# A hybrid mLSTM/RWKV-7 decoder step on one core: the scaled input kept in DRAM channel-major, the conditioning weight in wide rows, and pieces handed out more finely

## The chip, the cores and the metric

The kernel runs on one core of a Trainium2 chip. The metric is the device time of one execution in microseconds (us). TensorE (PE in the profile; PEld are its weight loads) does the matrix products, VectorE (DVE) and ScalarE (ACT) the elementwise work, GpSimd (POOL) small helpers, and SyncE (SP) issues all the DMAs, in order, from one queue.

## The reference, cut to what matters

One decoder layer for a prompt of 512 tokens and for 8 sequences of 4 sampled tokens, 1024 channels, in float32:

```python
mod = silu(c) @ w_cond + b_cond                      # [9, 6*1024]
sh1, sc1, g1, sh2, sc2, g2 = split(mod, 6)
h = x * (1 + sc1) + sh1
proj = h @ w_in                                      # mLSTM q, k, v, gates; RWKV r, k, v, LoRA; output gates
y_a = gate_a * head_norm(mlstm(proj)) * mlstm_norm_w   # 4 heads, matrix memory 256 x 256
y_b = (head_norm(rwkv7(proj)) * ... + bonus) * g       # 16 heads, state 64 x 64
y_mix = (y_a + gate_b * y_b) @ w_out
x1 = layer_norm(ALPHA * x + g1 * y_mix)
h2 = x1 * (1 + sc2) + sh2
x2 = layer_norm(ALPHA * x1 + g2 * (relu(h2 @ w_up)**2 @ w_down))
```

The nine rows of `mod` are the prompt's conditioning vector and those of the eight sequences. The outputs are `x2` for both groups and the final states.

## The kernel before

**Layout.** Activations lie channel-major: 128 channels on the partitions, the 32 sample tokens and then the 512 prompt tokens along the free dimension (T = 544; TX = 552 with 8 shift rows in front). Every projection is done in three float32r products: weight and activation are each split in a rounded part and a rest (`hi`, `lo`; ScalarE rounds, VectorE subtracts), and `mm3` (L313 to L315) adds hi*hi, hi*lo and lo*hi. `load_w` loads a weight block of 128 columns into the ring `wring` (two buffers, tile `wraw`) and splits it (L299 `whi`, L301 `wlo`).

**PSUM.** `psA` has two double banks (`big()`) for projections, `psB` four single banks (`tp()`) for everything else: transposes, small products, accumulators.

**Stages.**
1. *Load and conditioning.* `xp` (prompt) and `xs40` (shift rows and sample rows) are loaded and transposed with TensorE into `hf`. The part of `w_cond` for `sh1` and `sc1` (ci 0 to 7, blocks of 256 columns) comes in 16 loads of 512 KB, tile `craw`. `cond` (L339 and following) multiplies a block: 8 contraction tiles, dealt over four column groups of the array (g = 0 to 3, two tiles accumulated in each), a copy `crows`, and two products with `fold`, which sum the four groups and turn channels onto the partitions; VectorE adds the bias and writes `mod`. After each pair of blocks (i, 4 + i) two channel blocks of `hf` are scaled and shifted in place, and split to `hhi` and `hlo`. Behind this stands the first projection (`xsp`), ordered after the last product of `cond`.
2. *RWKV*, eight pairs of heads: `g_proj`, `g_prep`, `g_sample`, `g_inv`, `g_chain`, `g_gate`. `heads_sum` sums over the channels of a head: `parts_of` splits its argument (L562 ScalarE `shi`, L564 VectorE `slo`), then two products with `bones` for each half of the tokens (L568, L569). It is used in `g_prep`, for `sq` and for `bv`. `finish` writes the result of a pair to DRAM, `udr`.
3. *mLSTM*, four heads: `g_mproj`, `g_mcore`, `g_msample` (its accumulator `pacc` keeps a bank of `psB` open over many pieces). In the same stretch of time `g_cond` computes the rest of `mod`, one block of 256 columns at a time (ci 8 to 23): two loads of `craw` (`mp` has two buffers) and one call of `cond`.
4. *Start of the output product*, `g_end`: the pools of the first mLSTM half are closed (`mfront`), prompt and sample rows are loaded once more, `udr` is read back block by block (`uk`, one buffer) and split into `uhi`, `ulo`; in 8 groups of 4 + 1 transposes ALPHA*x is made channel-major, `xt` (L1487 to L1490), and then 12 products over the first 6 contraction tiles of `w_out` begin to add to `xt` (`residual`, L1461 to L1465).
5. *The rest of the output product, layer norm, MLP, layer norm*, written out in order.

**Order of the work.** Stages 2 to 4 are Python generators. Each `yield` gives a due time in nominal us, counted from the generator's base (PP for a pair of heads, MS for an mLSTM projection, CS_ for a conditioning block, ES for an output product); `merge` always resumes the generator whose next piece is due first, at once if its time is already past. So these times only set the program order of the pieces: they are no waits. The tile framework places semaphores and buffers, and may let a ready instruction go ahead of one that is not.

Of the kernel before, what the change touches and what calls it, by code (L numbers as in the profile page):

```python
# [41 lines left out]
def hybrid_kernel(ctx: ExitStack, tc: tile.TileContext, I, O):  # L42
# [127 lines left out]
    def load_x(pool, with_shift):  # L170
        xp = pool.tile([128, 4, D], F32, name="xp")
        dma(xp, I["x_prompt"].rearrange("o (n p) d -> p (o n) d", p=128))
        xs40 = pool.tile([40, D], F32, name="xs40")
        if with_shift:
            dma(xs40[0:NB, :], I["state_rwkv_shift"].rearrange("o b d -> (o b) d"))
        o = 8 if with_shift else 0
        for t in range(NT):
            dma(xs40[o + 8 * t:o + 8 + 8 * t, :], I["x_sample"][:, t, :])
        return xp, xs40
# [12 lines left out]
    def cond_load(ci, pool):  # L192
        raws = []
        for half in range(2):
            raws.append(pool.tile([128, 4, 256], F32, name="craw"))
            dma(raws[half], w_cond[:, 4 * half:4 * half + 4, 256 * ci:256 * ci + 256])
        return raws

    xp, xs40 = load_x(ep, True)
# [30 lines left out]
    for ci in (0, 4, 1, 5, 2, 6, 3, 7):  # L230
        if ci == 3:
            xraw = wring.tile([128, 8, 128], F32, name="wraw")
            dma(xraw, w_in[:, :, OFF_R + 128 * 24:OFF_R + 128 * 25])
        craws[ci] = []
        for half in range(2):
            raw = er.tile([128, 4, 256], F32, name="craw")
            with tc.high_priority() if (ci, half) in ((7,0),(7,1)) else ExitStack():
                dma(raw, w_cond[:, 4 * half:4 * half + 4, 256 * ci:256 * ci + 256])
            craws[ci].append(raw)
# [17 lines left out]
    hf = er.tile([128, 8, TX], F32, name="hf", bufs=1)  # L257
# [75 lines left out]
    def cond(cis, raws, rows, ps, nr=2):  # L333

        n = len(cis)
        for i, ci in enumerate(cis):
            for half in range(2):
                for g in range(4):
                    mm = PE.matmul(ps[32 * g:32 * g + 32, i, :], cth[:, 4 * half + g, :], raws[ci][half][:, g, :],  # L339
                                   start=half == 0, stop=half == 1)  # L340
        rw = rows.tile([128, n, 256], F32, name="crows", bufs=nr)
        S.copy(rw, ps)
        pt = tp([128, n, 2, 9])
        for i, ci in enumerate(cis):
            for j in range(2):
                PE.matmul(pt[:, i, j, :], rw[:, i, 128 * j:128 * j + 128], fold[:, 0:9], start=True, stop=True)
            V.tensor_tensor(mod[:, 2 * ci:2 * ci + 2, :], pt[:, i],
                            bcond[:, 2 * ci:2 * ci + 2].unsqueeze(2).to_broadcast([128, 2, 9]), op=ALU.add)
        return mm


    for i in range(4):
        if i == 3:
            xsp = split(xraw)
        mm = cond((i, 4 + i), craws, er, tp([128, 2, 256]))
        for k in (2 * i, 2 * i + 1):
            hp = hf[:, k, 40:TX]
            if k % 2 == 0:
                S.activation(hp, hp, AF.Identity, scale=mod[:, 8 + k, 0:1], bias=mod[:, k, 0:1])
            else:  # L360
                S.activation(hp, hp, AF.Identity, scale=mod[:, 8 + k, 0:1], bias=mod[:, k, 0:1])
            hv = hf[:, k, 8:40].rearrange("p (t b) -> p t b", b=NB)
            for o_, op in ((8, ALU.mult), (0, ALU.add)):
                V.tensor_tensor(hv, hv, mod[:, o_ + k, 1:9].unsqueeze(1).to_broadcast([128, NT, NB]), op=op)
            V.tensor_copy(hhi[:, k, :], hf[:, k, :])
            V.tensor_tensor(hlo[:, k, :], hf[:, k, :], hhi[:, k, :].bitcast(F32), op=ALU.subtract)
            S.copy(hl[:, k, 0:1], hf[:, k, TX - 1:TX])
            S.copy(hl[:, k, 1:9], hf[:, k, 32:40])
# [202 lines left out]
    def heads_sum(src):  # L571
        hi, lo = parts_of(src)
# [39 lines left out]
    PP = 53.34  # L612
# [35 lines left out]
    def g_prep(p, s):  # L648
# [5 lines left out]
        yield -1.39  # L654
# [69 lines left out]
        for i, c0 in enumerate((0, 4)):  # L724
            yield 14.83 + 3 * i
# [9 lines left out]
        yield 21.85  # L735
# [10 lines left out]
        yield 23.44  # L746
# [18 lines left out]
        yield -11.05  # L765
# [19 lines left out]
        ps = heads_sum(bv)  # L785
        need(("be", p - 2))
        for h, q in enumerate(halves):
# [4 lines left out]
            V.tensor_tensor(b_s[q, h, 1, :], km[q, 0:NS], cwf[q, NB:NB + NS], op=ALU.mult)  # L792
        V.tensor_tensor(two(bv), two(v_), pv(ps), op=ALU.mult)
# [27 lines left out]
    def g_inv(p, s):  # L821

        yield 29.19
# [19 lines left out]
        yield 45.69  # L843
# [3 lines left out]
        V.transpose(fl(t1), fl(x16))  # L847
        pt = tp([128, 8, 32])
# [38 lines left out]
    def g_chain(p, s):  # L887
        yield 45.34
# [37 lines left out]
        V.tensor_tensor(st, pn, wend.unsqueeze(2).to_broadcast([128, 8, 64]), op=ALU.mult)  # L926
        sc = scw2[p % 2]
# [6 lines left out]
        for c in range(8):  # L934
            yield 61.2 + 1.0 * c - 4.79
# [12 lines left out]
        yield 76.24  # L948
        pm = tp([128, NP])
        sum2(pm, bmean, *parts_of(o))  # L950
# [4 lines left out]
        yield 88.51  # L955
        pm = tp([128, NP])
        sum2(pm, bmean, *parts_of(o2))
# [33 lines left out]
    def g_sample(p, s):  # L991
# [26 lines left out]
        yield 37.83  # L1018
# [36 lines left out]
        yield 51.08  # L1055
# [95 lines left out]
    def g_mproj(h, s):  # L1151
# [16 lines left out]
        for j in range(2):  # L1168
# [5 lines left out]
            yield MS * (i - 0.2) + 1.67 - 7.39 + 5.82 + 9.07 - 0.12 + 2.38 + 5.52  # L1174
# [35 lines left out]
    def g_mcore(h, s):  # L1210
# [9 lines left out]
        for n in range(4):  # L1220
            yield n - 5.12 + 1.44 - 0.48 + 0.58 + 1.54 - 8.54 + 0.73 + 1.41
# [4 lines left out]
        yield 8.98  # L1226
# [22 lines left out]
        for j in range(4):  # L1249
            yield 6.05 + 3 * j + 10.0  # L1250
# [15 lines left out]
        for i in range(4):  # L1266
            yield 18.72 + 2 * i
# [20 lines left out]
        for j in range(2):  # L1288
            yield 26.8 + 2 * j
# [10 lines left out]
        yield 48.61  # L1300
# [8 lines left out]
    def g_msample(h, s):  # L1309
# [27 lines left out]
        for i in range(2):  # L1337
            css, cTs = [], []
            for g in range(4):
                yield 15.78 + 15 * i + 2 * g - 1.58  # L1340
# [12 lines left out]
            yield 8.91 + 15 * i  # L1353
# [21 lines left out]
        yield 41.57  # L1375
# [385 lines left out]
```

## Time and profile before

| | us |
|---|---|
| median of 3 runs | 1412.5 |
| the runs | 1402.83, 1413.77, 1412.5 |
| profiled execution | 1412.73 |
| its span in the trace | 1411.0 |

The mean granted clock of TensorE in the profiled execution was 0.97. A row of a table of stages has the stretch (us from the span's start), its length, the busy time and instruction count of PE, PEld, DVE, ACT and POOL, the granted clock, the mean busy share of the 16 DMA engines, and GB/s. A row of a timeline has start, length, engine, line and operation, written tile, read tiles, shapes, count, and in brackets the idle time before it with what ended it. A row of a group has line, engine, operation, count, busy time, mean ns of one, and the idle time before. A row of waits has who waited for whom, us in total, times, and the longest. The busy time of PE is a union of modelled lengths: matmuls are pipelined, so two that start 0.13 us apart can each be given 0.29 us.

### The profile page before, as it was taken

What the parts mean: (1) busy time and instruction counts of PE and PEld (TensorE: products, weight loads), DVE (VectorE), ACT (ScalarE), POOL (GpSimd) and SP (SyncE); (2) the same over time, 40 slices, a digit from 0 to 9 for tenths busy, and PEclk for the clock granted to TensorE, in tenths of its full rate; (3) what the DMA queues carried; (4) which work ended last, traced back from release to release, by engine and by line L of the source; (5) the groups of instructions that cost most, each with busy time, mean ns of one, the idle gap of its engine ahead of it and who ended that gap; (6) DMA issues with size and microseconds to landing.
All of it is one profiled execution on the core that took longest, in us unless ns stands there. A gap on an engine that the chain in (4) does not pass through costs nothing.

```text
span 1411.0 us, 29533 instructions
## 1 busy us (share of the span) xinstructions
PE 1329.0 (94%) x12048; PEld 1197.4 (85%) x12048; DVE 848.4 (60%) x2036; ACT 633.5 (45%) x1190; POOL 76.0 (5%) x308
## 2 busy tenths in 40 slices
PE   5988999999999999999999999899999999999996
PEld 3777878888787878898888887688899999999996
DVE  3487776967768676576457464387933343443446
ACT  2445556656566555465444444433831231322410
POOL 5100000000000000011010010000000000000000
PEclk9789999999999988999999999899999999999999
DMA  9522223122221221243754745553422333322321
GB/s 265 137 70 45 62 45 76 46 56 66 51 76 44 54 50 45 57 145 116 227 174 140 242 136 173 190 163 118 134 70 82 89 91 90 90 86 82 104 75 64
DMA packets 251482, 145.63 MB, mean 103 GB/s; under 512 B 52683, under 2 KB 244413, under 8 KB 251323
## 3 DMA queue, kind: packets, MB, share of 16 engines
q1 hardware_dynamic: 251347, 143.75, 36.0%
q8 instruction: 95, 1.56, 0.5%
q14 instruction: 40, 0.33, 0.1%
HBM read 124.58 MB, written 19.14 MB: 102 GB/s over the span
## 4 chain that ended last, share of the span: by engine, by line
PE 74%; DMA 8%; DVE 7%; ACT 7%; issue 3%; SPq 0%; POOLq 0%; POOL 0%; DVEq 0%; ACTq 0%
PE mm L313 18%; PE mm L314 18%; PE mm L315 17%; DMA craw<-in_w_cond_dram 3%; DVE wlo L301 2%; ACT whi L299 2%; PE tp L730 1%; PE tp L1258 1%; PE tp L339 1%; DMA wraw<-in_w_up_dram 1%; PE tp L900 1%; PE tp L938 1%; PE tp L1347 1%; PE tp L1270 1%; DMA wraw<-in_w_down_dram 1%
## 5 line engine op out<-in xcount | busy, mean ns | idle before, releaser
L313 PE MATMUL mm<-hhi,whi 128*128 128x272 f32 (+1 forms) x1712 | 509.1, 298 | 7.1 <-ACT aa L658 2.9
L314 PE MATMUL mm<-hlo,whi 128*128 128x272 f32 (+1 forms) x1712 | 505.7, 296 | 1.1 <-DVE hlo L1577 0.9
L315 PE MATMUL mm<-hhi,wlo 128*128 128x272 f32 (+1 forms) x1712 | 503.5, 294 | 1.0 <-DVE wlo L301 0.7
L313 PEld LDWEIGHTS mm<-hhi,whi 128*128 128x128 f32 x1712 | 326.8, 191 | 20.4 <-issue 7.6
L314 PEld LDWEIGHTS mm<-hlo,whi 128*128 128x128 f32 x1712 | 326.9, 191 | 7.3 <-issue 2.5
L315 PEld LDWEIGHTS mm<-hhi,wlo 128*128 128x128 f32 x1712 | 326.8, 191 | 3.7 <-issue 1.7
L299 ACT CAST whi<-wraw 128x1024 fp32r<-128x1024 f32 (+1 forms) x142 | 146.3, 1031 | 391.5 <-PE mm L314 381.0
L301 DVE TENSOR_TENSOR wlo<-wraw,whi 128x1024 fp32r<-128x1024 f32 (+1 forms) x142 | 170.4, 1200 | 130.3 <-ACT whi L299 129.8
L313 PE MATMUL mm<-hid,whi 128*128 128x272 f32 x384 | 110.8, 289 | 0.0
L315 PE MATMUL mm<-hid,wlo 128*128 128x272 f32 x384 | 110.6, 288 | 0.0
L314 PE MATMUL mm<-hil,whi 128*128 128x272 f32 x384 | 110.5, 288 | 0.0
L313 PEld LDWEIGHTS mm<-hid,whi 128*128 128x128 f32 x384 | 72.3, 188 | 0.6 <-ACT hid L1586 0.6
L314 PEld LDWEIGHTS mm<-hil,whi 128*128 128x128 f32 x384 | 72.3, 188 | 0.0
L315 PEld LDWEIGHTS mm<-hid,wlo 128*128 128x128 f32 x384 | 72.2, 188 | 0.0
L1461 DVE TENSOR_TENSOR g1s<-mm,mod 128x32 f32<-128x32 f32 x48 | 9.2, 191 | 104.2 <-PE mm L315 103.9
L1465 DVE SCALAR_TENSOR_TENSOR xt<-mm,mod,xt 128x240 f32<-128x240 f32 (+2 forms) x92 | 43.6, 476 | 8.9 <-PE mm L315 8.8
L1145 DVE SCALAR_TENSOR_TENSOR acc<-qr,chalf,acc 128x32 f32<-128x32 f32 (+1 forms) x96 | 43.9, 498 | 3.3 <-ACT acc L1143 2.9
L1586 ACT CAST hid<-rl 128x544 fp32r<-128x544 f32 (+1 forms) x37 | 21.7, 585 | 39.6 <-DVE rl L1585 39.6
L339 PE MATMUL tp<-craw,cth 128*32 128x256 f32 x384 | 31.4, 418 | 5.3 <-DMA craw<-in_w_cond_dram 5.2
L1587 DVE TENSOR_TENSOR hil<-rl,hid 128x544 fp32r<-128x544 f32 (+1 forms) x37 | 24.0, 648 | 19.5 <-ACT hid L1586 19.3
L831 DVE TENSOR_TENSOR itmp<-xi,ai 128x2 f32<-128x2 f32 (+14 forms) x120 | 29.9, 249 | 6.2 <-POOL ai L744 3.0
L1350 ACT COPY cT<-tp 128x512 f32<-128x512 f32 x32 | 18.0, 589 | 28.7 <-PE tp L1347 28.7
(546 smaller groups left out, 2221.0 us busy)
## 6 DMA issues: line engine op xcount, KB each, us to landing
wraw<-in_w_in_dram SPq DMA_DIRECT2D x66, 512.0 KB
craw<-in_w_cond_dram SPq DMA_DIRECT2D x48, 512.0 KB
wraw<-in_w_up_dram SPq DMA_DIRECT2D x32, 512.0 KB
wraw<-in_w_down_dram SPq DMA_DIRECT2D x32, 512.0 KB
cs<-in_state_mlstm_C_dram SPq DMA_DIRECT2D x32, 256.0 KB
out_C_s_dram<-cs SPq DMA_DIRECT2D x32, 256.0 KB
wraw<-in_w_out_dram SPq DMA_DIRECT2D x12, 384.0 KB
xp<-in_x_prompt_dram SPq DMA_DIRECT2D x2, 2048.0 KB
```

Source lines behind the costliest of these rows:

```text
L299: S.copy(hi, raw)
L301: V.tensor_tensor(lo, raw, hi.bitcast(F32), op=ALU.subtract)
L313: PE.matmul(out, hi[k], xhi[k], start=first and k == 0, stop=False)
L314: PE.matmul(out, hi[k], xlo[k], start=False, stop=False)
L315: PE.matmul(out, lo[k], xhi[k], start=False, stop=last and k == n - 1)
L339: mm = PE.matmul(ps[32 * g:32 * g + 32, i, :], cth[:, 4 * half + g, :], raws[ci][half][:, g, :], start=half == 0, stop=half == 1)
L831: V.tensor_tensor(tmp[:, 0:nq, 0:t + 1], xi[:, 0:nq, 0:t + 1], ai[:, 0:t + 1, t].unsqueeze(1).to_broadcast([128, nq, t + 1]), op=ALU.mult)
L1145: V.scalar_tensor_tensor(a, qr[:, base + j * step:base + j * step + n], w(j), a, op0=ALU.mult, op1=ALU.add)
L1350: S.copy(cT[:, :, 0:256], pt.rearrange("p a b c -> p a (b c)"))
L1465: V.scalar_tensor_tensor(d, ps[:, o:n], mod[:, goff + m, 0:1], d, op0=ALU.mult, op1=ALU.add)
L1586: S.copy(hid[:, f, a:a + n], rl)
L1587: V.tensor_tensor(hil[:, f, a:a + n], rl, hid[:, f, a:a + n].bitcast(F32), op=ALU.subtract)
```

## The change

**The scaled input.** In stage 1 the transposed rows now stay in `hf`, which moves to the longer-lived pool `ep`; scale and shift go into a small tile `ht` (POOL copies the 8 shift columns). Then POOL multiplies `hf` by ALPHA in place and eight DMAs write it to a new DRAM buffer `xdr`. In `g_end`, eight DMAs read `xt` from it; the second load of the input, the transposes and the ScalarE copies are gone. `uk` has two buffers.

**The conditioning weight.** It is loaded one contraction tile at a time: for stage 1 in two halves (512 columns of `sh1` and 512 of `sc1`, rows of 2 KB), later 1024 columns at once (rows of 4 KB). `cond_step` multiplies one contraction tile, the column groups g now holding different columns, and accumulates over the 8 tiles; `cond_end` copies, does two 128x128 transposes, and adds the bias in two instructions. `g_cond` runs four times (ci 2 to 5), and hands out load and product of each contraction tile separately; its PSUM bank is open from tile 0 to the end.

**The hand-out.** `parts_of` and the product that follows it become two pieces at `heads_sum` and at the head norms; so do `V.transpose` and the products behind it in `g_inv`, and the two halves of a step of `g_chain`. Some 30 due times are other numbers, among them PP. `g_end` opens at 21.96 instead of 8.46, and its products are due from 15.53 instead of 27.73 on.

```diff
     udr = dram1.tile([8, 128, T], F32)
+    xdr = dram1.tile([8, 128, T], F32)
...
+    for st_ in range(2):
+        for k in range(8):
...
+            raw = er.tile([128, 2, 512], F32, name="craw")
+            with tc.high_priority() if (st_, k) in ((1, 6), (1, 7)) else ExitStack():
+                dma(raw, w_cond[:, k, 0:2 * D].rearrange("p (a c) -> p a c", a=2)[:, :, 512 * st_:512 * st_ + 512])
...
+    def cond_step(ps, k, raw):
+        rv = raw.rearrange("p a (b c) -> p (a b) c", c=256)
+        for g in range(4):
+            mm = PE.matmul(ps[32 * g:32 * g + 32, :], cth[:, k, :], rv[:, g, :], start=k == 0, stop=k == 7)
+        return mm
+    def cond_end(ps, rows, mv, bv):
+        rw = rows.tile([128, 256], F32, name="crows")
         S.copy(rw, ps)
+        pt = tp([128, 2, 128])
+        for j in range(2):
+            PE.transpose(pt[:, j, :], rw[:, 128 * j:128 * j + 128], ident)
+        pv_ = pt.rearrange("p j (a b r) -> p a b j r", a=2, b=2)
+        for a in range(2):
+            V.tensor_tensor(mv[:, a], pv_[:, a, :, :, 0:9], bv[:, a].unsqueeze(3).to_broadcast([128, 2, 2, 9]), op=ALU.add)
...
+        for k in range(4 * st_, 4 * st_ + 4):
+            ht = er.tile([128, TX], F32, name="ht", bufs=2)
+            G.tensor_copy(ht[:, 0:8], hf[:, k, 0:8])
+            S.activation(ht[:, 40:TX], hf[:, k, 40:TX], AF.Identity, scale=mod[:, 8 + k, 0:1], bias=mod[:, k, 0:1])
...
+            V.tensor_copy(hhi[:, k, :], ht)
+            V.tensor_tensor(hlo[:, k, :], ht, hhi[:, k, :].bitcast(F32), op=ALU.subtract)
...
+            G.tensor_scalar(hf[:, k, 8:TX], hf[:, k, 8:TX], ALPHA, None, op0=ALU.mult)
+    for k in range(8):
+        dma(xdr[k], hf[:, k, 8:TX])
...
-    PP = 53.34
+    PP = 53.06
...
-        ps = heads_sum(sq)
+        hs_ = parts_of(sq)
         S.activation(lw, lw, AF.Copy, scale=CDEC, bias=CDEC)
...
+        yield -13.03 + 1
+        ps = heads_sum(*hs_)
...
-        ps = heads_sum(bv)
+        hs_ = parts_of(bv)
...
+        yield 35.19
+        ps = heads_sum(*hs_)
         V.tensor_tensor(two(bv), two(v_), pv(ps), op=ALU.mult)
...
-        yield 45.69
+        yield 47.85
...
         V.transpose(fl(t1), fl(x16))
+        yield 45.69 + 0.5
...
     def g_cond(ci):
-        yield -15.17
-        raws = cond_load(ci, M["mp"])
-        yield 23.57
-        cond((ci,), {ci: raws}, M["mp"], tp([128, 1, 256]))
+        def load(k):
+            raws[k] = M["mp"].tile([128, 2, 512], F32, name="craw")
+            dma(raws[k].rearrange("p a c -> p (a c)"), w_cond[:, k, 1024 * ci:1024 * ci + 1024])
+        for k in range(8):
+            yield -15.17 + CS_ * k / 2 + 15.51
+            load(k)
+            yield 22.8 + CS_ * (k - 1) / 2 - 4.64
+            if k == 0:
+                ps = tp([128, 256])
+            cond_step(ps, k, raws[k])
+        yield 22.8 + CS_ * 4
...
     def g_end():
-        yield 8.46
+        yield 21.96
         mfront.close()
...
+        for k in range(8):
+            dma(xt[:, k, :], xdr[k])
         lst = ExitStack()
-        lx = pool(lst, "lx")
-        xp, xs40 = load_x(lx, False)
+        lx = pool(lst, "lx", 2)
         for k in range(KA):
-            uk = lx.tile([128, T], F32, name="uk", bufs=1)
+            uk = lx.tile([128, T], F32, name="uk")
             dma(uk, udr[k])
             usplit(k, uk, slice(0, T))
-        for k in range(8):
-            yield 4.59 + 1.2 * k
-            ps = big()
-            for n in range(4):
-                PE.transpose(ps[:, 1, 128 * n:128 * n + 128], xp[:, n, 128 * k:128 * k + 128], ident)
-            PE.transpose(ps[:, 0, 0:NS], xs40[0:NS, 128 * k:128 * k + 128], ident[0:NS, 0:NS])
-            S.activation(xt[:, k, NS:T], ps[:, 1, :], AF.Copy, scale=ALPHA)
-            S.activation(xt[:, k, 0:NS], ps[:, 0, 0:NS], AF.Copy, scale=ALPHA)
...
         for i in range(8 + NA):
-            yield 24.7 + ES * i + 3.03
+            yield 24.7 + ES * i + 3.03 - 12.2
...
-    for ci in range(8, 24):
-        gens.append((MB + MP_ + 10 + CS_ * (ci - 8), g_cond(ci)))
+    for ci in range(2, 6):
+        gens.append((MB + MP_ + 10 + 4 * CS_ * (ci - 2), g_cond(ci)))
```

More of the change, by code (lines that the diff above doesn't have):

```diff
@@ L168, in hybrid_kernel @@
     udr = dram1.tile([8, 128, T], F32)
[L170 to L179, printed above, removed]
+    xdr = dram1.tile([8, 128, T], F32)
     early = ExitStack()
@@ L190, in hybrid_kernel @@
     w_cond = I["w_cond"].rearrange("o (k p) c -> p (o k) c", p=128)
[L192 to L199, printed above, removed]
+    xp = ep.tile([128, 4, D], F32)
+    dma(xp, I["x_prompt"].rearrange("o (n p) d -> p (o n) d", p=128))
+    xs40 = ep.tile([40, D], F32)
+    dma(xs40[0:NB, :], I["state_rwkv_shift"].rearrange("o b d -> (o b) d"))
+    for t in range(NT):
+        dma(xs40[8 + 8 * t:16 + 8 * t, :], I["x_sample"][:, t, :])
     craws = {}
@@ L229, in hybrid_kernel @@
     small.append((n0r, I["state_mlstm_n"].rearrange("o b h k -> (o b) (h k)")))
[L230 to L239, printed above, removed]
+    for st_ in range(2):
+        for k in range(8):
+            if (st_, k) == (1, 4):
+                xraw = wring.tile([128, 8, 128], F32, name="wraw")
+                dma(xraw, w_in[:, :, OFF_R + 128 * 24:OFF_R + 128 * 25])
+            raw = er.tile([128, 2, 512], F32, name="craw")
+            with tc.high_priority() if (st_, k) in ((1, 6), (1, 7)) else ExitStack():
+                dma(raw, w_cond[:, k, 0:2 * D].rearrange("p (a c) -> p a c", a=2)[:, :, 512 * st_:512 * st_ + 512])
+            craws[(st_, k)] = raw
             for x_ in small[:2]:
@@ L242, in hybrid_kernel @@
             small = small[2:]
+    assert not small
     gw = wring.tile([128, 8, 128], F32, name="wraw")
@@ L255, in hybrid_kernel @@
     S.activation(cth[:, :, 0:9], ps, AF.Copy, scale=0.5)
-    hf = er.tile([128, 8, TX], F32, name="hf", bufs=1)
+    hf = ep.tile([128, 8, TX], F32)
     for k in range(8):
@@ L330, in proj @@
         return proj_w(hi, lo, 0, 276, 276) if shifted else proj_w(hi, lo, 8, 272, 272)
[L333 to L341, printed above, removed]
-        S.copy(rw, ps)
[L343 to L349, printed above, removed]
@@ L352, in hybrid_kernel @@
-    for i in range(4):
-        if i == 3:
-            xsp = split(xraw)
[L355 to L368, printed above, removed]
+    def cond_step(ps, k, raw):
[3 more added lines that the diff above has]
+        return mm
@@ new lines, in hybrid_kernel @@
+    for st_ in range(2):
+        ps = tp([128, 256])
+        for k in range(8):
+            mm = cond_step(ps, k, craws[(st_, k)])
+        bv_ = bcond[:, 0:16].rearrange("p (a b) -> p a b", a=2)[:, :, 4 * st_:4 * st_ + 4]
+        cond_end(ps, er, m1v(mod, st_), bv_.rearrange("p a (b j) -> p a b j", j=2))
+        if st_ == 1:
+            xsp = split(xraw)
+        for k in range(4 * st_, 4 * st_ + 4):
+            ht = er.tile([128, TX], F32, name="ht", bufs=2)
+            G.tensor_copy(ht[:, 0:8], hf[:, k, 0:8])
+            S.activation(ht[:, 40:TX], hf[:, k, 40:TX], AF.Identity, scale=mod[:, 8 + k, 0:1], bias=mod[:, k, 0:1])
+            hv = ht[:, 8:40].rearrange("p (t b) -> p t b", b=NB)
+            V.tensor_tensor(hv, hf[:, k, 8:40].rearrange("p (t b) -> p t b", b=NB),
+                            mod[:, 8 + k, 1:9].unsqueeze(1).to_broadcast([128, NT, NB]), op=ALU.mult)
+            V.tensor_tensor(hv, hv, mod[:, k, 1:9].unsqueeze(1).to_broadcast([128, NT, NB]), op=ALU.add)
+            V.tensor_copy(hhi[:, k, :], ht)
+            V.tensor_tensor(hlo[:, k, :], ht, hhi[:, k, :].bitcast(F32), op=ALU.subtract)
+            S.copy(hl[:, k, 0:1], ht[:, TX - 1:TX])
+            S.copy(hl[:, k, 1:9], ht[:, 32:40])
+            G.tensor_scalar(hf[:, k, 8:TX], hf[:, k, 8:TX], ALPHA, None, op0=ALU.mult)
@@ L947, in g_chain @@
         s["sc"] = sc
-        yield 76.24
+        yield 75.9
+        hs_ = parts_of(o)
+        yield 76.24 + 0.7
         pm = tp([128, NP])
-        sum2(pm, bmean, *parts_of(o))
+        sum2(pm, bmean, *hs_)
         V.tensor_tensor(o, o, pm, op=ALU.subtract)
@@ L955, in g_chain @@
         yield 88.51
+        hs_ = parts_of(o2)
+        yield 88.51 + 0.7
         pm = tp([128, NP])
[L957 removed]
+        sum2(pm, bmean, *hs_)
         s.update(o=o, lt=lt, p=p)
@@ L1410, in g_cond @@
     def g_cond(ci):
-        yield -15.17
-        raws = cond_load(ci, M["mp"])
-        yield 23.57
-        cond((ci,), {ci: raws}, M["mp"], tp([128, 1, 256]))
+        ps = None
+        raws = {}
+        def load(k):
[6 more added lines that the diff above has]
+            if k == 0:
+                ps = tp([128, 256])
+            cond_step(ps, k, raws[k])
+        yield 22.8 + CS_ * 4
+        v5 = lambda a: a.rearrange("p (a b j) r -> p a b j r", a=2, b=2)
+        cond_end(ps, M["mp"], v5(mod[:, 8 * ci:8 * ci + 8, :]),
+                 bcond[:, 8 * ci:8 * ci + 8].rearrange("p (a b j) -> p a b j", a=2, b=2))
     def g_mouts():
```

54 lines of the change are left out of this document (29 added, 25 removed).

## The prediction

> **What bounds the kernel now.** I read the page first, for the busy shares and the chain that ended last, then one table of stages, then TensorE's waits.
>
> ```profile
> span 1411.0 us, 29533 instructions
> PE 1329.0 (94%) x12048; PEld 1197.4 (85%) x12048; DVE 848.4 (60%) x2036; ACT 633.5 (45%) x1190; POOL 76.0 (5%) x308
> PE 74%; DMA 8%; DVE 7%; ACT 7%; issue 3%; SPq 0%; POOLq 0%; POOL 0%; DVEq 0%; ACTq 0%
> ```
>
> TensorE is busy 94% of the span and carries 74% of the chain. So there are two ways to gain: take work away from TensorE, or close the 82 us (1411.0 - 1329.0) in which it idles. The table of stages (columns: stretch, its length, busy time and count of each engine, granted clock, DMA share, GB/s) says where they are:
>
> ```profile
> 0.00:62.00 62.00, 44.93 (x308) 32.70 (x309) 25.04 (x67) 18.77 (x47) 23.16 (x111) 0.83 0.76 215
> 62.00:180.00 118.00, 106.36 (x1055) 95.81 (x1053) 85.40 (x216) 63.27 (x116) 5.42 (x24) 0.94 0.26 61
> 180.00:600.00 420.00, 391.68 (x4710) 343.74 (x4709) 306.63 (x824) 241.56 (x487) 16.46 (x71) 0.97 0.23 56
> 600.00:890.00 290.00, 288.51 (x2230) 247.71 (x2228) 167.13 (x388) 143.73 (x276) 27.24 (x96) 1.00 0.57 175
> 890.00:985.00 95.00, 86.63 (x547) 72.08 (x547) 64.98 (x169) 36.24 (x72) 0.61 (x4) 0.93 0.46 139
> 985.00:1411.00 426.00, 410.88 (x3209) 405.39 (x3207) 199.24 (x375) 129.92 (x194) 3.09 (x2) 0.99 0.31 89
> ```
>
> Idle of TensorE by stage: 17.1 us in the load and conditioning stage, 11.6 in the start of the RWKV pairs, 28.3 in their steady part, 1.5 in the mLSTM stage, 8.4 around the start of the output product, 15.1 in the MLP. The change touches all but the last. In the mLSTM stage only removed TensorE work counts; elsewhere removed waits count as well.
>
> **Part 1, the output stage's residual.** Before, the prompt is loaded again at about 880 us, transposed on TensorE in 8 groups of 4 + 1, scaled on ScalarE. The timeline of TensorE there, first, second and last rows of the groups:
>
> ```profile
> 890.23 1.09 PE L1487 MATMUL mm<-ident,xp 128*128 128x128 f32 x8
> 895.69 0.42 PE L1488 MATMUL mm<-ident,xs 32*128 32x32 f32 x2 [4.37 <-DMA xs<-in_x_sample_dram]
> 896.77 1.12 PE L1487 MATMUL mm<-ident,xp 128*128 128x128 f32 x4 [0.67 <-ACT xt L1490]
> ...
> 900.64 0.69 PE L1347 MATMUL tp<-ident,cs 128*128 128x128 f32 x2
> ...
> 904.12 1.91 PE L1258 MATMUL tp<-q,k 128*128 128x512 f32 x2
> ...
> 906.59 0.24 PE L1488 MATMUL mm<-ident,xs 32*128 32x32 f32 x1
> ```
>
> The groups run from 890.23 to 906.83 us, 16.6 us. What else TensorE does in between is that L1258 row (1.7 us to the next transpose, 905.82) and four transposes of `cs` (two of them in the row at 900.64, 0.48 us to the next group at 901.12, and two single ones of 0.27); so 13.9 us go with the groups: their own work, the 4.37 us wait for the sample rows and 0.67 for ScalarE. The clock adds to it:
>
> ```profile
> 890.00:900.00 10.00, 4.82 (x24) 3.58 (x24) 3.65 (x6) 5.61 (x19) 0.00 (x0) 0.63 0.72 220
> 900.00:910.00 10.00, 10.00 (x40) 6.37 (x39) 2.94 (x5) 4.44 (x13) 0.00 (x0) 0.69 0.10 30
> ```
>
> After the idle the granted clock is 0.63 and 0.69 for 20 us, which slows what follows. All this is removed, with the 16 ScalarE copies. What is late next? The product needs `uhi` of six channel blocks, made from `udr`:
>
> ```profile
> 896.39 0.45 DVE L1191 CAST hhi<-uk 128x544 fp32r<-128x544 f32 x1 [3.81 <-DMA uk<-udr]
> 924.11 0.44 DVE L1191 CAST hhi<-uk 128x544 fp32r<-128x544 f32 x1 [1.14 <-DMA uk<-udr]
> ```
>
> With one `uk` buffer the six blocks take 896.39 to 925.3 us. With two, loads overlap the split of the block before. But 8 loads of `xt` now stand ahead of them in SP's queue (2.2 MB, as much as the 2.1 MB of `xp` and `xs` that they replace), and the first product is handed out right behind the loads, 5.8 nominal us earlier than before, where 19.3 nominal us lay between. TensorE may then wait for `uk`. Bounds: -16.6 (the whole stretch) and 0 (every us comes back as a wait for `uk`). I take **-12**, near the 13.9 of the rows, less a little for `uk`.
>
> The store that feeds this costs early time: 8 POOL multiplications of 128x544 and 8 stores of 272 KB. No row shows that POOL operation; the nearest are
>
> ```profile
> 4.37 0.52 POOL L119 MEMSET cmask<- 128x512 f32 x1
> 1.19 0.29 POOL masks.py:199 TENSOR_SCALAR_AFFINE_SELECT ident<-ident 128x128 f32<-128x128 f32 x1
> 50.00:55.00 5.00, 5.00 (x31) 5.00 (x30) 3.96 (x7) 2.03 (x7) 0.00 (x0) 0.70 0.06 6
> ```
>
> so 0.55 us each (by the memset) to 1.2 (by the select, scaled to 544 columns): 4 to 10 us in all, beside a TensorE busy all of 50 to 55 us, where POOL does nothing and the DMA engines are 0.06 busy. The 2.2 MB need some 8 us at the 270 GB/s of the rows in part 3. Behind the 8 stores in SP's queue stand the next `wraw` and `w2a` loads; they are asked for well ahead, so I cost it 0; if the cover is gone, the last store's wait for POOL delays a weight by up to 3 us.
>
> **Part 2, the late conditioning (ci 8 to 23).** Groups of TensorE by line in the mLSTM stage, 600 to 890 us:
>
> ```profile
> L339 PE MATMUL tp<-craw,cth 128*32 128x256 f32 x256 | 19.0, 387 | 1.3 <-DMA craw<-in_w_cond_dram 1.2
> L346 PE MATMUL tp<-fold,crows 128*128 128x9 f32 x64 | 8.8, 247 | 0.1
> ```
>
> The products stay 256 instructions, in 32 steps of 8 instead of 16 groups of 16. The timeline has a group of 8:
>
> ```profile
> 864.64 0.64 PE L339 MATMUL tp<-craw,cth 128*32 128x256 f32 x8
> ```
>
> So 32 x 0.64 = 20.5 us against 19.0: +1.5. The 64 fold matmuls (8.8 us) become 8 transposes at 0.28 us (four of L1487's take 1.12): 2.2 us, so -6.6. The loads get rows of 4 KB, and each buffer is freed one step earlier, so this stall of SP shrinks, off TensorE's path:
>
> ```profile
> SPq L50 <- PE tp L339: 47.0, 18, 9.4
> L1350 ACT COPY cT<-tp 128x512 f32<-128x512 f32 x32 | 18.0, 589 | 28.7 <-PE tp L1347 28.7
> ```
>
> The price: the accumulator of a conditioning block is open over 8 steps, so one of psB's four banks is nearly always held, and two for 11 of each 51 nominal us (step 0 of a block is due at 51 + 11.8 = 62.8, the one before closes at 73.8). `pacc` holds another. An evacuation such as the 0.59 us of L1350 can then hold TensorE up. By the code some 48 such tiles per head, 190 in all: 0 to 112 us. TensorE has projection matmuls to interleave and is idle only 1.5 us here; I take 2. Part 2: 1.5 - 6.6 + 2 = **-3**.
>
> **Part 3, the early conditioning.** Rows of 2 KB instead of 1 KB, and two halves of 512 channels instead of four quarters. By stretches:
>
> ```profile
> 5.00:10.00 5.00, 0.99 (x8) 0.93 (x8) 1.21 (x1) 0.70 (x2) 4.53 (x24) 1.00 1.04 368
> 25.00:30.00 5.00, 3.67 (x44) 2.50 (x44) 3.15 (x11) 2.38 (x7) 0.00 (x0) 1.00 1.03 274
> 44.11 1.08 PE L339 MATMUL tp<-craw,cth 128*32 128x256 f32 x8 [0.62 <-DMA craw<-in_w_cond_dram]
> ```
>
> The DMA engines are full: 368 GB/s while `xp` (4 KB rows) is moved, 274 with the 1 KB rows of `craw`. The last `craw` is used at 44.1 us. 8.39 MB take 30.6 us at 274 and 22.8 at 368; 2 KB rows lie nearer to the first, say 300: 28.0, so -2.6 (0 to -7.8). The Trainium skill (DMA: Bandwidth & Descriptors, Specifications) puts the minimum for line rate at 512 B; by it both widths run at line rate and the -2.6 is 0. The two rows above speak against it, but the xp stretch also holds other traffic.
>
> Against it, four channel blocks instead of two are modulated behind the last load. Per block VectorE has
>
> ```profile
> L366 DVE TENSOR_TENSOR hlo<-hf,hhi 128x552 fp32r<-128x552 f32 x8 | 5.8, 731 | 0.2
> 27.66 0.45 DVE L365 CAST hhi<-hf 128x552 fp32r<-128x552 f32 x1 [0.33 <-ACT hf L359]
> 26.81 0.52 DVE L364 TENSOR_TENSOR hf<-hf,mod 128x32 f32<-128x32 f32 x4
> ```
>
> 0.73 + 0.45 + 0.26 = 1.44 us, so +2.9 for two blocks; blocks 0 to 3 give TensorE 12 matmuls before it needs block 4, at the cold clock's spacing in the chain,
>
> ```profile
> 45.72 0.23 PE mm L314
> ```
>
> 2.8 us, which cover the 2.9 if they start with them. I cost half, +1.4. Part 3: **-1.2** (-8 to +3).
>
> **Part 4, the hand-out in the RWKV pairs.** TensorE's waits, 180 to 600 us (total, times, longest):
>
> ```profile
> PE mm L568 <- ACT shi L562: 11.1, 7, 1.7
> PE tp L860 <- issue: 3.9, 2, 2.6
> 244.92 0.39 PE L568 MATMUL mm<-shi,bones 128*128 128x272 f32 x1 [1.71 <-ACT shi L562]
> ```
>
> The largest is one place per pair: the head sum of `bv` waits for ScalarE's `shi`. The change puts 1.17 nominal us between the split (at 34.02) and the sum (35.19), so other pieces can be handed out between them. The head sum of `sq` gains nothing in time, since its new due time, -12.03, lies before the piece it follows (-8.67): only ScalarE's `lw` and the scan move ahead of it. `V.transpose` of `x16` is handed out later too (47.85 for 45.69). Some 30 other pieces move, and each can make a wait as well as close one; no row prices a move. Bounds: -40.0 (all idle of both RWKV stages closed, 11.6 + 28.3) and +11 (a second wait of the size of L568's). I take three quarters of that wait: **-8**.
>
> **Sum.** -12 - 3 - 1.2 - 8 = -24.2. The profiled execution took 1412.73 us around a span of 1411.0; the median of the runs is 1412.5, the fastest 1402.83. 1412.7 - 24.2 = **1388 us**, from 1378 to 1399 with the likely errors of the terms. A difference under 1%, 14 us, is about what a measurement of this kernel can't tell from none.
>
> **Rivals.**
> - The moved pieces bring new waits: part 4 is +4 instead of -8, the rest stands: -12.2, **1400 us**. For it: DVE is busy 306.63 of 420 us there and ACT 241.56, so a wait closed in one place easily opens at the next. Against: the wait is at one known place in each pair. 0.14.
> - The moved pieces close most idle: part 4 is -20 and the wide rows give -8 (part 3 -6.4): -41.4, **1371 us**. For it the 40 us of idle; against, that behind the one of 11.1 us every wait is under 4 us in total. 0.12.
> - Line rate at any row over 1 KB: the engines move 274 GB/s either way, part 3 is +1.4, sum -21.6, **1391 us**. For it: the DMA share is 1.03 in the 1 KB stretch and 1.04 with `xp`. 0.08. (This is the rule of the Trainium skill weighed in part 3.)
> - The change doesn't do what it says at the output stage: `xt` and `uk` wait in SP's queue behind weights, TensorE stands as long as it did with the transposes, part 1 is 0: -12.2, **1400 us**. For it, the uk row's 3.81 us wait. 0.06.
> - Slower: psB. With one or two banks held by open conditioning sums and one by `pacc`, each of the 190 tiles of the mLSTM stage waits for its evacuation. At 0.14 us a tile (26.2 us, part 2's allowance of 2 among it) the gain is eaten, at 0.22 us (over a third of 0.59) it is 42 - 26.2 = +16: **1428 us**. Against: projection matmuls lie between most tiles. 0.08.
>
> The forecast keeps 0.52. **Range and chances.** 1400 and 1371 have to be inside; up to about 1412, where the psB wait just eats the gain, and down to 1368: 0.08 above and some 0.06 below are left out. Faster by over 1% (under 1398): 0.52 + 0.12 + 0.08 = 0.72. Within 1%: 0.14 + 0.06 = 0.20. Slower: 0.08.
>
> **What would show it.** Part 1: no transposes of `xp` after 880 us, granted clock near 1.00 in the 20 us at 890, no wait for `xs`, `uk` done within 20 us. Part 2: line L346's 64 matmuls gone, TensorE's idle in the mLSTM stage still under 4 us; psB waits would show as TensorE waiting for ACT `cT` or DVE. Part 3: last `craw` product at 41 us, not 44. Part 4: the wait on `shi` under 3 us. I am wrong if TensorE stands at the first output product for `uk`, or if idle in 180 to 600 us is not below 24 us.

## The result and the profile after

The changed kernel takes 1371.75 us (median of four runs, 1367.72 to 1373.65), the one before 1412.42 in the same series: a ratio of 0.9724, 95% interval 0.9683 to 0.9765, that is -40.7 us where -24.2 was forecast. Its profiled execution took 1371.71 us around the span below. The three lines of the page after that answer to those of before:

```profile
span 1369.7 us, 29267 instructions
PE 1302.4 (95%) x11924; PEld 1168.1 (85%) x11924; DVE 849.7 (62%) x2024; ACT 611.5 (45%) x1154; POOL 93.7 (7%) x324
PE 73%; DVE 10%; DMA 6%; ACT 5%; issue 4%; SPq 1%; POOL 1%; POOLq 0%; DVEq 0%; ACTq 0%
```

TensorE is still the bound. Its busy time fell by 26.6 us (1329.0 to 1302.4), its idle time by 14.7 (82.0 to 67.3). Three rows of the table of stages after, columns as before:

```profile
0.00:62.00 62.00, 42.95 (x318) 28.65 (x319) 28.57 (x64) 19.88 (x49) 35.09 (x117) 0.89 0.80 252
...
180.00:600.00 420.00, 406.20 (x4925) 357.96 (x4925) 325.27 (x847) 258.14 (x519) 21.52 (x85) 0.99 0.27 66
600.00:890.00 290.00, 287.21 (x2135) 236.40 (x2134) 168.09 (x391) 125.47 (x253) 23.01 (x84) 0.99 0.59 183
```

Idle in the steady RWKV stretch fell from 28.3 to 13.8 us, and 4925 products were counted in the same 420 us instead of 4710: the stage got faster, it was not only refilled. The stores of the RWKV states, one for each pair of heads, and of the mLSTM states, one for each head, date the stages (row: count, shortest, median and longest ns of one, first and last start). Before, then after:

```profile
L50 SPq DMA_DIRECT2D out_S_p_dram<-so x8: 612/632/665, 209.9 to 608.6; - x8
L50 SPq DMA_DIRECT2D out_C_p_dram<-cp x4: 372/604/1364, 687.5 to 945.8; - x4
```

```profile
L50 SPq DMA_DIRECT2D out_S_p_dram<-so x8: 612/630/665, 202.7 to 580.2; - x8
L50 SPq DMA_DIRECT2D out_C_p_dram<-cp x4: 383/390/395, 657.4 to 909.2; - x4
```

At the first pair's store after is 7.2 us ahead, at the eighth 28.4, at the last head's 36.6, and 41.3 at the end of the span (1411.0 to 1369.7). So some 28 of the 41 us were gained up to the end of RWKV and 13 behind it; the forecast had 9 (parts 3 and 4) and 15 (parts 1 and 2). TensorE's waits in 180 to 600 us after (total, times, longest):

```profile
PE mm L302 <- ACT aa L657: 2.4, 5, 0.5
PE tp L774 <- ACT gk L765: 2.3, 5, 0.5
...
PE tp L568 <- ACT shi L562: 1.3, 1, 1.3
```

The 11.1 us on `shi` (seven times on an `mm` tile) are gone; what is left is 1.3 us, once, on a `tp` tile, which is another sum. It looks as if the split had done what it was meant to; the experiments say that it had not.

### The profile page after: what moved, and what is told of

Same layout as the page of the kernel before. It is cut to its first block, busy times and chain, and to the rows that moved or that the text cites. A ratio compares the mean times of both kernels' runs of the same rounds, so it can differ in the third digit from the quotient of the medians.

```text
span 1369.7 us, 29267 instructions
## 1 busy us (share of the span) xinstructions
PE 1302.4 (95%) x11924; PEld 1168.1 (85%) x11924; DVE 849.7 (62%) x2024; ACT 611.5 (45%) x1154; POOL 93.7 (7%) x324
## 4 chain that ended last, share of the span: by engine, by line
PE 73%; DVE 10%; DMA 6%; ACT 5%; issue 4%; SPq 1%; POOL 1%; POOLq 0%; DVEq 0%; ACTq 0%
PE mm L302 17%; PE mm L303 17%; PE mm L304 17%; DMA craw<-in_w_cond_dram 2%; PE tp L326 2%; DVE wlo L290 1%; PE tp L1279 1%; PE tp L1267 1%; PE tp L1356 1%; PE tp L904 1%; PE tp L1294 1%; DMA wraw<-in_w_down_dram 1%; PE tp L1373 1%; PE mm L555 1%; PE tp L943 1%
## 5 line engine op out<-in xcount | busy, mean ns | idle before, releaser
L302 PEld LDWEIGHTS mm<-hhi,whi 128*128 128x128 f32 x1712 | 324.9, 190 | 26.6 <-issue 11.8
L326 PE MATMUL tp<-craw,cth 128*32 128x256 f32 x384 | 37.8, 424 | 8.5 <-DMA craw<-in_w_cond_dram 8.5
```

Of the source, the lines that this page charges most:

```text
L302: PE.matmul(out, hi[k], xhi[k], start=first and k == 0, stop=False)
L326: mm = PE.matmul(ps[32 * g:32 * g + 32, :], cth[:, k, :], rv[:, g, :], start=k == 0, stop=k == 7)
```

## Experiments

All are timed against the kernel before; a ratio's 95% interval stands in brackets.

**1 and 2. The hand-out alone, and all but the hand-out.** The edit is the whole of part 4: the due times and splits of the RWKV generators, put in or left as before.

> The kernel before with the whole hand-out of the RWKV pairs as after the change (the split sums, all due times of the pairs, PP); input, conditioning, mLSTM and output start as before. Theory A, from the two traces: the pairs' period went from 59.4 to 55.7 us and the stage gave some 25 us, all from the hand-out: about 1387 us, 1383 to 1392. Rival B, the prediction's step: the hand-out closes three quarters of the one wait on shi, 8 us: about 1404 us. Rival C: the pairs got shorter because something else left them (the conditioning's or the output stage's effect on queues): no gain here, 1412.

> The kernel after the change with the RWKV pairs handed out as before (old due times and PP, sums not split); everything else as after. Theory A: gives back some 25 us: about 1397 us. Rival B: gives back 8 us: about 1380. Rival C: gives back nothing, 1372.

Alone: 1381.41 us against 1410.27, ratio 0.9782 [0.9748, 0.9815], -29 us. All but it: 1394.37, ratio 0.9884 [0.9835, 0.9933], -16 us. The two add up to -45, four more than the whole. So the hand-out is worth 23 to 29 us, not 8, and the rest 10 to 16, where the forecast's other three terms add up to 16.2. In the second run the old wait is back:

```profile
PE mm L568 <- ACT shi L562: 11.0, 7, 1.7
```

**3. The split of the `bv` sum alone**, the step on which the forecast's -8 rested:

```diff
-        ps = heads_sum(bv)
+        hs_ = parts_of(bv)
...
+        yield 35.19
+        ps = heads_sum(*hs_)
```

> The kernel before with one edit: the head sum of bv is handed out 1.17 nominal us behind its split. Prediction's step: the wait on shi (11.1 us in 180 to 600 us, 1.7 each) falls by three quarters, 8 us off: about 1404 us. Rival A1: the split alone moves too little work in between, the wait stays over 1 us a pair, gain under 3 us: 1410 or more.

1443.44 us, ratio 1.021 [1.0162, 1.0258]: 33 us slower. Its waits and its stretch of 180 to 600 us:

```profile
PE mm L555 <- DVE bv L794: 15.3, 6, 2.6
PE tp L1041 <- ACT zt L1037: 7.9, 6, 2.1
180.00:600.00 420.00, 383.69 (x4222) 328.79 (x4221) 288.88 (x782) 225.32 (x453) 14.44 (x63) 0.90 0.21 51
```

The wait on `shi` is gone, but the LoRA products (L555) now wait for the `bv` product on VectorE, which must empty the sum's double bank of psA, and the sample pieces wait for `zt`. The granted clock falls to 0.90.

**4. Only the `ar`·`bk` products earlier:**

```diff
-            yield 14.83 + 3 * i
+            yield 14.83 + 3 * i - 22.76
```

> The kernel before with one edit: the products of ar and bk (32 TensorE instructions a pair, four psB tiles, masked by VectorE) are due at -7.93 instead of 14.83. In the traces their group went from 2.96 us busy and 0.54 idle a pair to 2.06 and none. Theory A2: this alone gives 1.4 us a pair, 11 us in all: about 1401 us. Rival: they only wait at another place for a bank or for bk, under 3 us: 1410 or more.

1394.46 us, ratio 0.9869 [0.9827, 0.9912]: -16 us from one number, more than the 11 expected, with the wait on `shi` still there:

```profile
PE mm L568 <- ACT shi L562: 10.2, 6, 1.7
180.00:600.00 420.00, 396.08 (x4802) 349.31 (x4801) 313.33 (x813) 250.47 (x501) 19.93 (x77) 0.98 0.24 58
```

TensorE's idle in this stretch fell only from 28.3 to 23.9 us. Where the rest of the 16 us comes from is not shown.

**5. The same number put back in the changed kernel** (ar·bk due at 14.83 again, all else changed):

> The kernel after the change with one edit: the products of ar and bk are due at 14.83 again instead of -7.93. Theory A: the 16 us that this move gave alone are given back: 1384 to 1390 us. Rival B: in the new order they find the banks free at either place, the loss is under 5 us: 1372 to 1377 us.

1494.58 us, ratio 1.057 [1.0538, 1.0601]: 123 us slower than the changed kernel, far more than either theory gave.

```profile
PE mm L302 <- DVE xr L528: 15.2, 5, 3.5
PE tp L876 <- DVE t L869: 12.6, 5, 2.9
180.00:600.00 420.00, 358.82 (x3633) 310.06 (x3629) 246.31 (x688) 202.26 (x399) 13.45 (x46) 0.86 0.19 46
```

`t` (L869) belongs to the pair's inverse, whose input goes from these products through DRAM. The moved times form one arrangement: a piece that is worth 16 us on its own is worth 123 once the others count on it.

**6. The `bv` sum joined again in the changed kernel:**

```diff
-        hs_ = parts_of(bv)
+        ps = heads_sum(*parts_of(bv))
...
-        yield 35.19
-        ps = heads_sum(*hs_)
```

> The kernel after the change with one edit: the head sum of bv stands again right behind its split. Theory A, the prediction's step in its new setting: the wait on shi, 1.6 us a pair, comes back, about 11 us: 1383 us, 1379 to 1386. Rival B: with all other pieces moved the wait no longer costs anything, or the shorter hold of the double psA bank (which made the split alone 33 us slower) repays it: 1370 to 1375 us.

1374.45 us, ratio 0.9732 [0.9711, 0.9753], 2.7 us more than the changed kernel and within its interval. The wait on `shi` does not come back. Why, the timeline shows. ScalarE before, around the sum of the pair that the prediction quotes:

```profile
239.66 1.05 ACT L299 CAST whi<-wraw 128x1024 fp32r<-128x1024 f32 x1 [5.46 <-PE mm L314]
...
242.69 1.51 ACT L780 COPY za<-tp 64x256 f32<-64x256 f32 x4
244.22 0.65 ACT L562 CAST shi<-bv 128x544 fp32r<-128x544 f32 x1
```

ScalarE works without a gap from 239.66 on; `shi` stands there behind nine other instructions and is ready at 244.87, while TensorE had only short pieces left after 239.58 (a head norm, transposes, LoRA products). With the sum joined, ScalarE and then TensorE:

```profile
234.47 1.05 ACT L288 CAST whi<-wraw 128x1024 fp32r<-128x1024 f32 x1 [2.08 <-PE mm L303]
...
238.44 1.50 ACT L781 COPY za<-tp 64x256 f32<-64x256 f32 x4
239.96 0.65 ACT L562 CAST shi<-bv 128x544 fp32r<-128x544 f32 x1
```

```profile
245.14 0.29 PE L304 MATMUL mm<-hhi,wlo 128*128 128x276 f32 x1
245.27 0.28 PE L568 MATMUL mm<-shi,bones 128*128 128x272 f32 x1
```

The same pieces in ScalarE's queue, but the sum now stands behind a projection block in TensorE's order (from 239.06 on) and comes 4.7 us after `shi` is ready (245.27 - 240.61). In the kernel before, the next projection block began at 245.15, behind the sum. What closed the wait in the changed kernel is a projection moved ahead of it, not a gap between split and sum. Which of the due times moved it there was not tried.

**7. ar·bk earlier and the split, without the rest:**

> The kernel before with two edits of the hand-out: ar·bk due 22.76 nominal us earlier, and the bv sum split with its own due time 35.19. Alone they gave -16 us and +33 us. Theory A: the split is harmful only while ar·bk is late, because then VectorE is behind when its bv product must free the double bank; with ar·bk early the split takes the wait on shi away (10.2 us in all, in the kernel with ar·bk early alone) and the two together give -24 to -29 us, nearly all of the hand-out's gain: about 1381 to 1386 us, wait on shi under 3 us, no wait on bv over 3 us in total. Rival B: the split needs the other moves too; the two effects add up, -16 + 33 = +17: about 1428 us, with TensorE waiting for bv and zt again.

1413.84 us, ratio 1.001 [0.9991, 1.003]: neither theory's number, nearer to "the effects add up". The split still costs some 19 us against experiment 4.

```profile
PE tp L1041 <- ACT zt L1037: 12.6, 6, 2.1
PE tp L939 <- DVE st L940: 6.1, 6, 2.4
PE mm L555 <- DVE bv L794: 4.9, 6, 0.8
```

**8. The moves in projection and preparation only** (PP, `g_proj` 4.05 earlier, `g_prep` with ar·bk, `za` and both splits of head sums; inverse, chain, gate and sample pieces as before):

> The kernel before with the part of the hand-out that lies in the projections and in the preparation of a pair (PP, the due times of g_proj and g_prep with ar·bk, and both splits of head sums); the inverse, the chain, the gate and the sample generators keep their old due times and pieces. All of the hand-out alone gave -29 us, ar·bk alone -16, ar·bk with the bv split +1. Theory A: the split pays only where the pieces that use the result lie elsewhere as well; with the old times of chain and sample TensorE waits for zt and st as in the run with ar·bk and the split (12.6 and 6.1 us there), so this kernel stays within 10 us of the one before: 1400 to 1420 us, with zt or st among the three largest waits. Rival B: the moves in projection and preparation make up most of the gain and the rest is worth under 10 us: 1381 to 1391 us, pair period under 57 us, neither zt nor st over 4 us in total.

1381.09 us against 1417.08, ratio 0.975 [0.9706, 0.9794]: all of the hand-out's gain, so theory A falls. (The kernel before was slower in this series than in experiment 1's, 1410.27; the two ratios, 0.975 and 0.9782, lie within each other's intervals.)

```profile
PE mm L313 <- ACT aa L657: 2.9, 6, 0.5
PE tp L941 <- DVE st L929: 1.4, 6, 0.3
180.00:600.00 420.00, 408.50 (x4896) 358.75 (x4895) 320.82 (x832) 259.00 (x518) 21.07 (x83) 0.99 0.27 66
```

The finer pieces and moved times in inverse, chain, gate and sample bring nothing that can be measured on top of these. Against experiment 7, seven more edits (PP, the projections' time, `za`, the other preparation steps and the split of the `sq` sum) turn +1 into -36; which of them does it was not tried one by one.

**9. The late conditioning as before, in the changed kernel** (16 blocks of 256 columns, one piece each, fold products):

> The kernel after the change with the late conditioning as before (16 blocks of 256 columns, rows of 1 KB, fold products); early conditioning and all else as after. Theory A, from the traces (an mLSTM head takes 86.1 us instead of 91.2): it carries most of that, some 12 us: 1384 us. Rival B, the prediction's term: 3 us: 1375 us. Rival C: the open psB bank costs more than the removed products bring: under 1369 us.

1376.64 us, ratio 0.9746 [0.972, 0.9772]: 4.9 us more than the changed kernel, nearer to rival B's 3 than to A's 12, but the intervals overlap. The profiled execution does not settle it by its length alone: its last RWKV state store comes at 585.4 us, 5.2 later than in the changed kernel, although the first late conditioning product of this run starts only at 634.7. Kernels with the same RWKV pieces (this one, the changed one, and the next three) have that store between 576.0 and 585.4. So a difference of 5 us between two of these kernels says little.

What lies behind RWKV can be compared without that spread, by counting from the first mLSTM head's state store to the end of the span. These stores in this run and in those of experiments 10 and 12 (the row of the changed kernel stands above):

```profile
L50 SPq DMA_DIRECT2D out_C_p_dram<-cp x4: 383/384/384, 661.1 to 919.8; - x4
L50 SPq DMA_DIRECT2D out_C_p_dram<-cp x4: 383/389/395, 657.0 to 907.6; - x4
L50 SPq DMA_DIRECT2D out_C_p_dram<-cp x4: 372/372/372, 655.0 to 906.5; - x4
```

In the changed kernel it is 712.3 us from the first of them to the end (1369.7 - 657.4). Two other runs with the same pieces behind RWKV agree: 712.6 (1395.3 - 682.7, experiment 2) and 713.3 (1373.6 - 660.3, experiment 11). In this run it is 717.3 (1378.4 - 661.1), 4 to 5 us more; from the first head's store to the last it is 258.7 against 251.8, and 258.3 in the kernel before. So the late conditioning is worth 4 to 5 us, on one execution of each kernel.

**10. The output start as before, in the changed kernel** (second load, transposes, old due times of `g_end`; no multiplication by ALPHA and no stores in stage 1):

> The kernel after the change without the scaled input in DRAM: the output stage loads and transposes the input again, with its old due times and one uk buffer, and the early stage neither multiplies by ALPHA nor stores. Theory A, the prediction's term: 12 us back, 1384 us (1380 to 1388). Rival B: the stage's wait for weights takes the place of the transposes, under 5 us: 1372 to 1377 us.

1378.01 us, ratio 0.976 [0.9739, 0.978]: 6.3 us where 12 were forecast. From the first head's store to the end it is 719.3 us (1376.3 - 657.0), 6 to 7 more than in the three runs named above, which agrees. The group of the transposes in this run (count, busy us, mean ns, idle before), two rows of its timeline, and the wait behind them:

```profile
L1512 PE MATMUL mm<-ident,xp 128*128 128x128 f32 x32 | 5.2, 285 | 0.8 <-ACT xt L1515 0.7
L1513 PE MATMUL mm<-ident,xs 32*128 32x32 f32 x8 | 1.8, 241 | 0.0
```

```profile
864.45 0.31 PE L1513 MATMUL mm<-ident,xs 32*128 32x32 f32 x2
867.08 0.66 PE L1512 MATMUL mm<-ident,xp 128*128 128x128 f32 x4
...
905.84 0.57 PE L302 MATMUL mm<-hhi,whi 128*128 128x272 f32 x1 [3.47 <-DVE xt L1486]
```

Four transposes take 0.66 us here, not 1.12, and the 4.37 us wait for the sample rows is absent: from 853.50 to 864.45 other pieces run between the first transposes of `xp` and those of `xs`. The stage costs 7.0 us of products (5.2 + 1.8) and 0.8 of waiting.

**11. Rows of 1 KB in the early conditioning**, in the changed kernel:

```diff
-            raw = er.tile([128, 2, 512], F32, name="craw")
+            raw = er.tile([128, 4, 256], F32, name="craw")
...
-                dma(raw, w_cond[:, k, 0:2 * D].rearrange("p (a c) -> p a c", a=2)[:, :, 512 * st_:512 * st_ + 512])
+                dma(raw, w_cond[:, k, 0:2 * D].rearrange("p (b e c) -> p e b c", b=4, e=2)[:, st_])
```

> The changed kernel, but the early conditioning weight is loaded in rows of 1 KB (four pieces of 256 columns for each contraction tile) in place of 2 KB; to do so, stage 0 makes the channel blocks 0, 1, 4, 5 and stage 1 the blocks 2, 3, 6, 7, and the first projection adds up its contraction tiles in that order. Theory A (the forecast's): the row width sets the rate, so the last early craw product, at 41.65 us in the changed kernel and 44.11 in the one before, comes at 44 us again, and the rate in the first 62 us falls from 252 towards 215 GB/s; total +2 to +3 us. Rival B (line rate at both widths): the last product stays within 0.7 us of 41.65 and the total within 1 us; the 2.5 us then came from the order of the loads and the smaller tail behind them.

1375.04 us, ratio 0.9738 [0.9709, 0.9766]. The last early product, in the changed kernel and then here:

```profile
41.65 1.08 PE L326 MATMUL tp<-craw,cth 128*32 128x256 f32 x8 [0.30 <-DMA craw<-in_w_cond_dram]
```

```profile
43.79 1.08 PE L326 MATMUL tp<-craw,cth 128*32 128x256 f32 x8 [0.42 <-DMA craw<-in_w_cond_dram]
```

2.1 us: theory A's date holds, though the rate in the first 62 us is 247 GB/s and not near 215. Stretches while the weight streams show it better, rows of 2 KB and then of 1 KB (the last three columns are clock, DMA share and GB/s):

```profile
30.00:35.00 5.00, 2.52 (x23) 0.56 (x24) 4.80 (x10) 2.20 (x6) 5.00 (x6) 0.57 1.04 305
35.00:40.00 5.00, 2.77 (x24) 0.40 (x16) 2.08 (x3) 1.04 (x1) 2.02 (x4) 0.50 0.99 360
```

```profile
30.00:35.00 5.00, 1.43 (x12) 0.40 (x16) 4.80 (x10) 2.48 (x10) 5.00 (x6) 0.59 1.06 268
35.00:40.00 5.00, 2.39 (x24) 0.40 (x16) 2.37 (x3) 1.04 (x1) 2.54 (x4) 0.50 1.06 327
```

The engines are no less full with the short rows and move 10% less: (268 + 327) against (305 + 360).

**12. The mLSTM due times as before**, in the changed kernel (ten numbers of the mLSTM generators):

> The changed kernel with the ten due times of the mLSTM generators as before; all else as changed. Theory A (remainder): of the 13 us that the changed kernel gains between the end of the RWKV pairs and the MLP, the late conditioning gave some 5 and the output start some 6, so the due times carry 2 to 3: about 1374 us, TensorE's idle in the mLSTM stage rises from 2.8 us by as much. Rival B: as with ar·bk, one moved piece decides; without the moves the output product waits for the mLSTM results or the eight conditioning steps collide with the chunks: +10 us or more, with a wait over 5 us at one place between 600 and 960 us.

1367.34 us, ratio 0.9684 [0.9657, 0.9711]: the lowest time of all, and against both theories. The interval overlaps the changed kernel's, and 4.2 us of the difference stand in the trace by the last RWKV store (576.0 against 580.2). Counted from the first head's store this run has 710.5 us (1365.5 - 655.0), about 2 less than the 712.3 to 713.3 of the three runs named above, and a wait of 3.1 us for `xt` near 905 us, which the changed kernel has and the kernel before has not, is absent. So the ten new numbers bring no gain and seem to cost some 2 us, on one execution of each kernel.

## Why the prediction was right and wrong

The time fell inside the range and on the forecast's side; the sum was 16 us short. It landed on the second rival's number, 1371, "the moved pieces close most idle", which had 0.12. That the number agrees so closely is luck: the rival's -20 for part 4 is near the truth, but its -6.4 for the wide rows is not, and it shares the -12 of part 1. All of the shortfall is in part 4; the other three terms, -16.2 together, measured 10 to 16.

- **Part 4, the hand-out: -8 forecast, -23 to -29 measured.** The step that failed is "the change puts 1.17 nominal us between the split and the sum, so other pieces can be handed out between them": by itself that costs 33 us, and taking it out of the changed kernel costs 2.7. The prediction took the largest wait for the prize and the edit beside it for the cause. It left the ar·bk products, moved by 22.76, among "some 30 other pieces" without a price; they alone are -16. By experiment 8 the projection and preparation times carry the whole term. The bound of -40 held, but it counts idle time alone, and idle is not all that the order sets. From the first pair's store to the sixth, before and then after:

```profile
209.90:506.96 297.06, 278.09 (x3409) 244.84 (x3397) 222.98 (x601) 175.62 (x350) 9.84 (x44) 0.98 0.24 58
202.71:481.22 278.51, 270.37 (x3418) 236.47 (x3408) 221.94 (x599) 173.97 (x350) 9.79 (x44) 1.00 0.26 62
```

  Of the 18.6 us gained here, 10.8 are idle time of TensorE (19.0 to 8.1) and 7.7 are shorter busy time for about as many products, at a granted clock of 1.00 against 0.98.
- **Part 1, the output start: -12 forecast, 6 measured.** Transposes, the wait for `xs` and the cold clock at 890 are gone, and the granted clock in these 20 us is 1.00 and 0.90. (The output start itself now lies some 35 us earlier; there, in 850 to 860 and 860 to 870 us, the clock is 0.84 and 0.99.)

```profile
890.00:900.00 10.00, 10.00 (x54) 8.65 (x52) 7.68 (x28) 1.85 (x6) 0.00 (x0) 1.00 0.44 135
900.00:910.00 10.00, 6.88 (x43) 5.85 (x42) 8.86 (x24) 1.24 (x3) 0.00 (x0) 0.90 0.28 79
855.86 0.44 DVE L1200 CAST hhi<-uk 128x544 fp32r<-128x544 f32 x1 [0.53 <-DMA uk<-udr]
...
872.71 0.71 DVE L1201 TENSOR_TENSOR hlo<-uk,hhi 128x544 fp32r<-128x544 f32 x1
```

  `uk` is split within 17.6 us (the last two rows), under the 20 named, and TensorE does not stand for it. The term was mis-sized because it was priced in the old surroundings: of the 13.9 us, 5.0 were waits and the transposes ran at a clock of 0.63 to 0.69. With the rest of the change in place the same code costs 7.0 us of products and 0.8 of waiting, because other pieces stand where the wait was (experiment 10); which edit brought them there is not shown. A wait for `xt` at 905 us, the idle 3.1 us in the row of 900 us, stands in the changed kernel and in experiment 10's run (3.47 us); the kernel before and experiment 12's run do not have it, so it seems to go with the new mLSTM due times.
- **Part 2, the late conditioning: -3 forecast, 4 to 5 measured (experiment 9).** Its own rows:

```profile
L326 PE MATMUL tp<-craw,cth 128*32 128x256 f32 x256 | 24.7, 389 | 0.2 <-DMA craw<-in_w_cond_dram 0.2
L335 PE MATMUL tp<-ident,crows x8: 270/272/476, 683.8 to 857.0; 128*128 128x128 f32 x8
```

  The steps of 8 products take 24.7 us against a forecast of 20.5 and 19.0 before, the 8 transposes 2.2 as forecast against 8.8. So these rows give only -0.9 (5.7 - 6.6) where -5.1 was forecast (1.5 - 6.6); where the rest of the measured gain comes from is not shown. The psB rival did not happen: TensorE is idle 2.8 us in 600 to 890, under the 4 named. One wait there, 0.8 us, is for the emptying of a bank of psB (`kw`, L1234), and experiment 9's run, which has no conditioning sum open over 8 steps, has it too.
- **Part 3, the early conditioning: -1.2 forecast, -3 where it acts, not settled later.** The last product comes 2.5 us earlier (44.11 to 41.65), as forecast (2.6), and 2.1 of them go with the width of the rows (experiment 11). The +1.4 for four blocks behind the last load did not show: in the run without the hand-out (experiment 2) four transposes behind the first projections come at 91.0 us, 94.3 before. Whether these 3 us last to the end cannot be read from the traces: that run stores the first pair's state at 209.7 us against 209.9, but the eighth at 605.4 against 608.6, while the eighth store comes at 580.4 with the hand-out alone and at 580.2 with the whole change. Differences of this size are within the spread of that store named in experiment 9.

  The Trainium skill's rule (DMA: Bandwidth & Descriptors, Specifications), line rate from 512 B on, by which the wide rows would give 0, does not fit experiment 11's 10%. The ALPHA multiplication on POOL was outside the bounds given, and no wait of TensorE in the trace is for it:

```profile
L366 POOL TENSOR_SCALAR hf<-hf x8: 1564/1751/1882, 28.8 to 52.3; 128x544 f32<-128x544 f32 x8
SPq L50 <- POOL hf L366: 7.0, 3, 3.1
```

  1.75 us each, 14 in all, where 0.55 to 1.2 were estimated. SP's queue waits for it 7.0 us in three places, the longest 3.1, about the 3 us that the prediction allowed.

By the forecast's measures: `shi` under 3 us, idle in 180 to 600 below 24, last `craw` product at 41, all as named. They were met while the reason given for one of them was false, which only undoing that step alone could show.

## What to carry to other kernels

A wait names the piece that came last, not the edit that will close it: look at what stands ahead of that piece in the order of both engines, and price each moved piece by where its results are needed next. Test a due time both alone and taken back from the whole: here one number was worth 16 us one way and 123 the other. And price removed work at the speed that it will have once the neighbouring stalls are gone, not at the speed of the stalled trace.

## What the runs showed of the hardware

The granted clock went with TensorE's idle time. In 180 to 600 us, TensorE's idle time (420 less its busy time) and its clock: 11.5 us and 0.99 (experiment 8), 13.8 and 0.99 (after), 28.3 and 0.97 (before), 36.3 and 0.90 (experiment 3), 61.2 and 0.86 (experiment 5). The total alone does not set the clock: experiment 7 has 34.8 us and 0.95, experiment 3 about the same idle and 0.90. The stretches hold different numbers of products, and no run held one of the two fixed while the other changed; but in the changed kernel less waiting came with shorter busy time for about as many products (7.7 us of 18.6, under part 4), so a wait's length in the trace is not its whole price.

The second point is the width of DMA rows: 10% of the rate between 1 KB and 2 KB, with the engines' busy share at 1.06 for the shorter rows against 0.99 to 1.04 (experiment 11).
